# A causal depthwise convolution as three filters of half the taps, in a two-layer streaming encoder on one core

## The chip, the core and the metric

The kernel runs on one core of a Trainium2 chip. The metric is the device time of one execution in microseconds (us). The core has a matrix engine (TensorE, PE in the profile, with its weight loads as PEld), a vector engine (VectorE, DVE), an engine for functions of one input (ScalarE, ACT), a general engine (GpSimd, POOL) and a queue for transfers (SyncE, SP). Each executes its own list of instructions in order and waits at semaphores for the others.

## The reference, cut to what matters

One step of a two-layer encoder over 576 frames: 512 of a new stream and 64 of a running one. Each layer projects its input to queries, keys, values and the two inputs of a convolution, runs attention and the convolution, projects both back, normalizes, and runs a feed-forward part with a second norm. The part that the change touches is the causal depthwise convolution with 31 taps over 512 channels, and what follows it:

```
CONV_WIDTH = 31; CONV_HIST = CONV_WIDTH - 1

def causal_depthwise_conv(u, hist, w, b):
    full = jnp.concatenate([hist, u], axis=1)
    y = lax.conv_general_dilated(full, w[:, None, :], window_strides=(1,), padding='VALID', ...,
                                 feature_group_count=D_CONV)
    return y + b, full[:, -CONV_HIST:]
...
    u = ca * jax.nn.sigmoid(cg)
    c, conv_state = causal_depthwise_conv(u, hist, p['conv_w'][l], p['conv_b'][l])
    c = jax.nn.silu(layer_norm(c, p['conv_ln_g'][l], p['conv_ln_b'][l]))
    mix = jnp.concatenate([attn.reshape(B, T, D_ATTN), c], axis=-1)
    y = jnp.einsum('bte,ed->btd', mix, p['w_out'][l])
```

## The kernel before

Activations lie with the channels on the 128 partitions and the 576 frames along the free dimension, in two groups of 288. A weight of 128x1024 comes in float32 and is split into a high and a low part (`wh`, `wl`); a product is three matmuls (lines 734, 735, 736: high by high, high by low, low by high) on blocks of 128x128 by 128x288. `weights` makes the split: ACT copies the high part (line 891), and DVE or POOL subtracts it for the low part (line 894); or, where the running fraction `DM` says so, ACT writes the negative and the high part (lines 875 and 881), and a DMA from POOL's queue adds the weight to the negative (line 878). Layer 1's first 20 weights are split ahead, during layer 0's feed-forward part, and kept in memory (`split_ahead`).

Per layer the work is: 20 projection units (queries q, keys k, values v, and the gate g and input a of each of four channel tiles of the convolution); rotary products (lines 1367 to 1385); attention for four heads, five query blocks each (lines 1486 to 1574); the convolution of four channel tiles; its layer norm over channels (sum over tiles at line 1669, mean by a matmul at 1679, scale at 1725); the output projection with the residual (lines 1799, 1804, 1857, running sums at 1835); a layer norm (`layer_norm`: mean at 1029 and 1034, subtraction at 1052, squares on ACT at 1058 with sums on POOL at 1064, statistics at 1006); the feed-forward part by a scheme with fewer block products; and the second norm.

The convolution of a tile reads `ub`, 636 columns: 30 zeros, the 512 frames, 30 frames of history and the 64 frames. All 606 windows are computed for each tap. The first `NPT` taps go over ACT, which multiplies by the tap (lines 1319 and 1322), and POOL, which adds (line 1325) into a tile `r`. The other taps go over DVE: one instruction of 606 elements each multiplies and adds into an accumulator in PSUM (`sc`, line 1337, the first tap at 1335). Three additions join the two (line 1344).

The order of all instructions on PE, DVE, ACT, POOL and SP is made ahead, when the program is built, by a list scheduler (`Sched`). It gives each step a cost per engine (`cV`, `cA`, `cG`, `cP`, `cD`), a priority, and buffers to take and return, and it picks the engine where several can do a step. Its numbers per phase (`PHASES`, four phases in each layer) set priorities, penalties and choices, `NPT` among them.

Of the kernel before, what the change touches and what calls it, by code (L numbers as in the profile page):

```python
# [144 lines left out]
DL = 2.2  # L145
# [56 lines left out]
  'LD1': 0.76,
  'LD2': 0.58,
  'LD3': 1.12,
  'LDO': 113.7,
# [4 lines left out]
  'PA': 729.8,  # L210
  'PC': -623.4,
  'PCN': 616.8,
  'PE_': 162.9,
  'PK': -234.5,
# [2 lines left out]
  'PR': -253.2,
  'PS': 120.4,
  'PT': 791.6,
  'PV': 358.4,  # L220
# [101 lines left out]
 {'CH': 2,  # L322
  'CSTD': 2,
  'DM': 0,
# [4 lines left out]
  'LD1': 1.27,  # L329
  'LD2': 2.31,  # L330
  'LD3': 1.29,
  'LDO': -40.7,
# [1 line left out]
  'LP': -1.01,
  'LPE': 0.85,
  'LPT': -0.43,
  'NPT': '9,10,12,12',
# [1 line left out]
  'PC': -524.7,
  'PCN': 602.4,  # L340
  'PE_': 461.1,
  'PK': -255.4,
  'PN': -270.8,
# [2085 lines left out]
```

## Time and profile before

| | |
|---|---|
| median of 3 runs | 1374.9 us (1372.52 to 1377.28) |
| the profiled execution | 1375.67 us, span 1373.9 us |
| busy: PE, DVE, ACT, POOL | 1308.0, 1078.1, 705.1, 302.3 us |
| granted clock of TensorE, mean | 0.977 |

The span runs from the first to the last instruction; the execution's own time is 1.8 us longer. An engine's busy time is a sum over stages with different limits, so the stretches matter more than the shares: projection, attention and convolution take about 35 to 210 us in layer 0 and 700 to 875 us in layer 1, and the feed-forward parts about 300 to 665 and 960 to 1345 us. The granted clock is 1.00 or 0.50 at each moment, and its mean over a stretch says what part of it ran at half.

### The profile page before, as it was taken

The numbers are of one execution on the slowest core, as the hardware profiler recorded it, in microseconds if no ns is written. First come the engines' busy times: TensorE is split into PE (matmuls) and PEld (weight loads), VectorE is DVE, ScalarE is ACT, GpSimd is POOL, SyncE is SP. The second block draws the span as 40 slices with busy tenths as digits, with TensorE's granted clock in tenths as the row PEclk, the third lists the DMA queues.
The fourth block names the chain that finished last, engine by engine and source line by source line (L and its number), as shares of the span: only waits on it lengthen the run. The fifth ranks groups of instructions, "written<-read, shape, count | busy, mean of one in ns | idle before, by whom it ended". The sixth has DMA issues, their size and how long they took to land.

```text
span 1373.9 us, 24858 instructions
## 1 busy us (share of the span) xinstructions
PE 1308.0 (95%) x9518; PEld 1264.1 (92%) x9518; DVE 1078.1 (78%) x2206; ACT 705.1 (51%) x1413; POOL 302.3 (22%) x292
## 2 busy tenths in 40 slices
PE   8989989979999999999999999899989999999997
PEld 7878879979899999999998988798889999999996
DVE  5899998777888887878658999868677676767737
ACT  5766677265444444434156657754654443434424
POOL 0456620150000000000144885223400000000013
PEclk9999989989999999999999999899999999999998
DMA  6635533334465645554345444454234343435262
GB/s 220 162 94 140 122 117 106 93 130 156 144 211 165 208 168 192 185 167 139 102 158 204 160 152 121 129 135 118 64 79 117 112 108 108 124 80 144 70 152 69
DMA packets 70102, 186.38 MB, mean 136 GB/s; under 512 B 10848, under 2 KB 16608, under 8 KB 69984
## 3 DMA queue, kind: packets, MB, share of 16 engines
q1 hardware_dynamic: 63504, 161.20, 34.9%
q0 software_dynamic: 6480, 23.60, 10.4%
q8 instruction: 75, 1.23, 0.4%
q14 instruction: 43, 0.35, 0.1%
HBM read 154.11 MB, written 30.65 MB: 134 GB/s over the span
## 4 chain that ended last, share of the span: by engine, by line
PE 72%; DVE 18%; issue 3%; DMA 2%; ACT 2%; POOL 2%; SPq 0%; ACTq 0%; DVEq 0%; POOLq 0%
PE b L734 21%; PE b L735 21%; PE b L736 21%; DVE sc L1337 8%; DMA raw<-in_wu_dram 2%; PE sc L734 1%; PE b L1006 1%; POOL sq L1064 1%; PE sc L736 1%; PE b L1568 1%; PE sc L735 1%; DVE nm L1486 1%; DVE P L1530 1%; DMA wl<-in_wu_dram 1%; PE b L1611 1%
## 5 line engine op out<-in xcount | busy, mean ns | idle before, releaser
L734 PE MATMUL b<-x,wh 128*128 128x288 f32 x1356 | 416.2, 307 | 6.6 <-ACT wh L891 4.0
L736 PE MATMUL b<-x,wl 128*128 128x288 f32 x1356 | 406.1, 299 | 7.0 <-DVE wl L894 4.8
L735 PE MATMUL b<-x,wh 128*128 128x288 f32 x1356 | 406.5, 300 | 1.7 <-DVE x L1215 1.1
L734 PE MATMUL b<-a,wh 128*128 128x288 f32 x1088 | 325.0, 299 | 0.2 <-ACT x L731 0.2
L735 PE MATMUL b<-a,wh 128*128 128x288 f32 x1088 | 321.3, 295 | 0.0
L736 PE MATMUL b<-a,wl 128*128 128x288 f32 x1088 | 321.0, 295 | 0.0
L734 PEld LDWEIGHTS b<-x,wh 128*128 128x128 f32 x1356 | 260.5, 192 | 13.5 <-ACT wh L891 4.0
L736 PEld LDWEIGHTS b<-x,wl 128*128 128x128 f32 x1356 | 260.2, 192 | 8.2 <-DVE wl L894 5.3
L735 PEld LDWEIGHTS b<-x,wh 128*128 128x128 f32 x1356 | 260.6, 192 | 4.0 <-DVE x L1215 2.5
L734 PEld LDWEIGHTS b<-a,wh 128*128 128x128 f32 x1088 | 205.1, 188 | 2.0 <-issue 0.6
L735 PEld LDWEIGHTS b<-a,wh 128*128 128x128 f32 x1088 | 205.4, 189 | 0.5
L736 PEld LDWEIGHTS b<-a,wl 128*128 128x128 f32 x1088 | 205.1, 188 | 0.0
L2273 DVE TENSOR_TENSOR r<-r,b 128x288 f32<-128x288 f32 x192 | 85.7, 450 | 87.6 <-PE b L736 87.3
L1337 DVE SCALAR_TENSOR_TENSOR sc<-ub,par,sc 128x606 f32<-128x606 f32 x160 | 136.2, 851 | 4.2
L878 POOL DMA_DIRECT2D wl<-in_wu_dram x45 | 39.2, 871 | 446.8 <-ACT wl L875 387.6
L1064 POOL TENSOR_TENSOR sq<-sq,sq 128x288 f32<-128x288 f32 x40 | 35.7, 910 | 416.1 <-ACT sq L1058 415.5
L1325 POOL TENSOR_TENSOR r<-r,prod 128x606 f32<-128x606 f32 x72 | 113.7, 1580 | 54.8 <-ACT prod L1322 31.0
L891 ACT CAST wh<-raw 128x1024 fp32r<-128x1024 f32 (+1 forms) x73 | 71.4, 979 | 71.2 <-PE b L735 52.3
L2056 ACT CAST wh<-ckv 128x512 fp32r<-128x512 f32 x104 | 64.1, 620 | 76.7 <-PE b L735 61.2
L894 DVE TENSOR_TENSOR wl<-raw,wh 128x1024 fp32r<-128x1024 f32 (+1 forms) x73 | 84.5, 1161 | 22.3 <-ACT wh L891 21.7
L1884 DVE TENSOR_TENSOR wl<-ckv,wh 128x512 fp32r<-128x512 f32 x104 | 71.1, 685 | 6.0 <-ACT wh L2056 5.8
L875 ACT ACTIVATE wl<-raw 128x1024 fp32r<-128x1024 f32 x45 | 47.7, 1060 | 44.2 <-PE b L736 25.5
(320 smaller groups left out, 2409.9 us busy)
## 6 DMA issues: line engine op xcount, KB each, us to landing
raw<-in_wu_dram SPq DMA_DIRECT2D x110, 512.0 KB, 4.6
wl<-in_wu_dram POOLq DMA_DIRECT2D x45, 512.0 KB, 7.2
wscr<-cs SPq DMA_DIRECT2D x80, 256.0 KB, 2.0
ckv<-in_wu_dram SPq DMA_DIRECT2D x26, 512.0 KB, 3.6
ah<-in_wu_dram SPq DMA_DIRECT2D x26, 512.0 KB, 4.4
cs<-in_wu_dram SPq DMA_DIRECT2D x40, 256.0 KB, 2.8
wh<-wscr SPq DMA_DIRECT2D x20, 512.0 KB, 3.3
wl<-wscr SPq DMA_DIRECT2D x20, 512.0 KB, 4.4
```

Of the source, the lines that this page charges most:

```text
L734: TE.matmul(o, wh, xh, start=start, stop=False)
L735: TE.matmul(o, wh, xl, start=False, stop=False)
L736: TE.matmul(o, wl, xh, start=False, stop=stop)
L875: S.activation(wt["lo"], wt["raw"], AF.Copy, scale=-1.0)
L891: S.copy(wt["hi"][:, c], wt["raw"][:, c])
L894: e.tensor_tensor(wt["lo"][:, c], wt["raw"][:, c], wt["hi"][:, c].bitcast(F32), op=ALU.subtract)
L1064: e.tensor_tensor(q[a]["t"], q[a]["t"], q[b]["t"], op=ALU.add)
L1325: GP.tensor_tensor(cc[t], cc[t], st[j], op=ALU.add)
L1337: V.scalar_tensor_tensor(st["a0"], win(j), w, st["a0"], op0=ALU.mult, op1=ALU.add)
L1884: e.tensor_tensor(o, a, b, op=ALU.subtract)
L2056: S.copy(tl["wh"][box["i"]][:, off:off + n], src())
L2273: V.tensor_tensor(rr, rr, bk(), op=ALU.add)
```

## The change

The convolution is computed with even and odd frames apart. With U0 and U1 the even and odd columns of `ub` (318 each), H0 the 16 even taps and H1 the 15 odd taps, it makes A = H0 on U0, B = H1 on U1 (with the bias), and C = (H0 + H1) on U0 + U1; the even outputs are A + B, and the odd ones C - A - B, with B taken one column later. That is 16 + 15 + 16 = 47 filters' taps over 303 or 304 columns, in place of 31 taps over 606, which is 62 in the same unit. B is made by ACT (products) and POOL (sums); `NPT` is at least 15 in the phases that use it, so all of B goes there. A and C are made on DVE, in the two banks of the same PSUM tile `sc`. C starts from the negative of A, which lies there. The sum U0 + U1 is a step for DVE or POOL. The results lie with the even outputs first, and the copies behind the convolution's norm put them back in order. `ub` is returned when A, B and U0 + U1 are made.

The scheduler's numbers are changed in all eight phases, with three of its constants (`PD`, `DL`, the cost of the first loads of x). The core of the diff:

```
-  'DM': 0.67,
+  'DM': 1,
...
-  'NPT': '9,9,9,10',
+  'NPT': '15,15,15,15',
...
+            taps = pr[:, P_CW:P_CB].rearrange("p (t w) -> p t w", w=W)
+            V.tensor_tensor(cv[:, :, 1:], taps[:, :, 2::2], taps[:, :, 1::2], op=ALU.add)
+            V.tensor_scalar(cv[:, :, 0], pr[:, P_CB:P_CG], 2.0, None, op0=ALU.mult)
...
+            def frames(odd, i, n):
+                return ub[t].rearrange("p (n two) -> p two n", two=2)[:, odd, i:i + n]
+            def b_(n=YH + 1, o=0):
+                return cc[t][:, UH + o:UH + o + n]
...
-                        S.activation(st[j], ub[t][:, j:j + UC], AF.Copy, scale=w)
+                        S.activation(st[j], frames(1, j, YH + 1), AF.Copy, scale=w)
...
-                    GP.tensor_tensor(cc[t], cc[t], st[j], op=ALU.add)
+                    GP.tensor_tensor(b_(), b_(), st[j], op=ALU.add)
...
+                e.tensor_tensor(cc[t][:, :UH], frames(0, 0, UH), frames(1, 0, UH), op=ALU.add)
+            sm = op({"V": cV(UH), "G": cG(UH)}, both, (*start, cc["n", t]), pri=PT)
...
-            for j in range(npt, W):
+            for j in range(W // 2 + 1):
...
-                        V.scalar_tensor_tensor(st["a0"], win(j), w, st["a0"], op0=ALU.mult, op1=ALU.add)
-                vt = op({"V": cV(UC, True) + 0.06}, va, (*start, pd, vt), acq=("cv", "sc") if j == npt else (), pri=PT)
+                        V.scalar_tensor_tensor(st["a"], frames(0, j, YH), w, st["a"], op0=ALU.mult, op1=ALU.add)
+                vt = op({"V": cV(YH, True)}, va, (*start, pd, vt), acq=("cv", "sc") if j == 0 else (), pri=PT)
...
+            for j in range(W // 2 + 1):
+                def vc(e, j=j):
+                    w = cv[:, t, j:j + 1] if j else pr[:, cw:cw + 1]
+                    V.scalar_tensor_tensor(st["c"], cc[t][:, j:j + YH], w, st["c"] if j else st["a"], op0=ALU.mult,
+                                           op1=ALU.add if j else ALU.subtract)
+                vt = op({"V": cV(YH, True)}, vc, (sm, vt, ld_n), pri=PT)
...
+                for o, i, n in ((0, 0, SEQ // 2), (SEQ // 2, S0 // 2, DEC // 2)):
+                    V.tensor_tensor(cc[t][:, o:o + n], st["a"][:, i:i + n], b_(n, i), op=ALU.add)
+                for o, i, n in ((0, 0, SEQ // 2), (SEQ // 2, S0 // 2, DEC // 2)):
+                    V.scalar_tensor_tensor(cc[t][:, T // 2 + o:T // 2 + o + n], st["c"][:, i:i + n], cv[:, t, 0:1],
+                                           b_(n, i + 1), op0=ALU.add, op1=ALU.subtract)
...
-                copy(e, cmix[t][0], cc[t][:, :T])
+                copy(e, halves(cmix[t][0]), cc[t][:, :T].rearrange("p (two n) -> p two n", two=2))
```

What the new numbers do to the order is seen in the instruction lists. VectorE in layer 0, the middle of the first tile's convolution, before (`ub` the tile's input, `par` the taps, `nm`, `rc` and `P` of attention):

```order
L1337 SCALAR_TENSOR_TENSOR sc_119<-ub_544,par_161,sc_119 128x2x303 x3
L1485 MEMSET sc_118 64x2x64
L1486 TENSOR_REDUCE nm_594<-sc_118 128x2
L1337 SCALAR_TENSOR_TENSOR sc_119<-ub_544,par_161,sc_119 128x2x303 x7
L1485 MEMSET sc_118 64x2x64
L1486 TENSOR_REDUCE nm_595<-sc_118 128x2
L1337 SCALAR_TENSOR_TENSOR sc_119<-ub_544,par_161,sc_119 128x2x303 x2
```

and now, from the end of the even filter into the summed one (`r` holds U0 + U1, `cv` the summed taps):

```order
L1524 TENSOR_REDUCE nm_588<-sc_118 128x2
L1367 SCALAR_TENSOR_TENSOR sc_119<-ub_538,par_161,sc_119 128x303 x2
L736 COPY ah_99<-b_117 128x128
L1374 SCALAR_TENSOR_TENSOR sc_119<-r_91,par_161,sc_119 128x303
L1374 SCALAR_TENSOR_TENSOR sc_119<-r_91,cv_165,sc_119 128x303
L1555 RECIPROCAL rc_593<-sums_587 128x2
L1556 TENSOR_TENSOR rc_593<-rc_593,nlam_162 128x1
L1374 SCALAR_TENSOR_TENSOR sc_119<-r_91,cv_165,sc_119 128x303 x2
L1568 SCALAR_TENSOR_TENSOR P_659<-P_659,rc_593 128x256
```

The taps are more instructions and half as wide, and attention's steps stand between them as before.

PE in layer 0 at the mean of the convolution's norm (`sgm` by `ones_h`), before; `x` by `wh` or `wl` are matmuls of the projection:

```order
L734 MATMUL b_115<-x_185,wh_85 128x288
L735 MATMUL b_115<-x_186,wh_85 128x288
L736 MATMUL b_115<-x_185,wl_89 128x288
L1539 MATMUL b_114<-ident,P_1783 128x128 x3
L1679 MATMUL sc_118<-sgm_101,ones_h 128x288 x2
L734 MATMUL b_115<-x_171,wh_85 128x288
L735 MATMUL b_115<-x_172,wh_85 128x288
L736 MATMUL b_115<-x_171,wl_89 128x288
```

and now:

```order
L740 MATMUL b_115<-a_1542,a_1299 128x64
L741 MATMUL b_115<-a_1541,a_1300 128x64
L1606 MATMUL b_116<-ah_99,a_1480 128x256 x3
L1606 MATMUL b_116<-ah_99,a_1480 128x128
L1717 MATMUL sc_118<-sgm_101,ones_h 128x288 x2
L739 MATMUL b_117<-x_181,wh_83 128x288
L740 MATMUL b_117<-x_182,wh_83 128x288
L741 MATMUL b_117<-x_181,wl_87 128x288
```

The mean stands after 806 matmuls of 288 columns instead of 890. In layer 1 it is 5102 instead of 5150, counted from the start of the program.

VectorE around the first layer norm of layer 0, before, from the last subtractions of the second group (`b_115` is its mean) to its statistics (`lrv`):

```order
L1052 TENSOR_TENSOR r_93<-r_93,b_115 128x288
L1052 TENSOR_TENSOR r_96<-r_96,b_115 128x288
L1052 TENSOR_TENSOR r_91<-r_91,b_115 128x288
L894 TENSOR_TENSOR wl_87<-raw_81,wh_83 128x1024
L894 TENSOR_TENSOR wl_88<-raw_82,wh_84 128x1024
L819 TENSOR_TENSOR cs_3077<-cs_3077 128x512
L959 TENSOR_SCALAR lrv_2936<-b_115 96x3
```

and now, from the last subtractions of the first group (`b_117`) to its statistics:

```order
L1066 TENSOR_TENSOR r_96<-r_96,b_117 128x288
L1066 TENSOR_TENSOR r_97<-r_97,b_117 128x288
L1838 SCALAR_TENSOR_TENSOR r_92<-r_92,b_114 128x288
L1838 SCALAR_TENSOR_TENSOR r_96<-r_96,b_116 128x288
L908 TENSOR_TENSOR wl_87<-raw_81,wh_83 128x1024
L1838 SCALAR_TENSOR_TENSOR r_97<-r_97,b_115 128x288
L1843 TENSOR_TENSOR r_96<-r_96,x_2494 128x288
L973 TENSOR_SCALAR lrv_3058<-b_117 96x3
```

The low part of the first feed-forward weight (`wl_87`) stood behind the second group's subtractions and now stands ahead of the first group's statistics. The second unit's low part (`wl_88`), which stood beside it, is now made by the accumulating DMA.

Counted over the whole program, DVE has 44 weight splits of 128x1024 instead of 65, POOL issues 66 accumulating DMAs instead of 45, and ACT has 66 negatives instead of 45 and as many high parts as before. In layer 0, ahead of its first norm: ten of those splits on DVE become five; seven more of the rotary steps at lines 1370, 1371 and 1385 stand on DVE and as many fewer on POOL; the 13 residual additions at line 1804 and the six sums at line 1835 that stood on DVE stand on POOL. In layer 1's same part, nine more additions, products and subtractions of 512 or 576 columns stand on DVE that stood on POOL, with two products of 64 columns.

More of the change, by code (lines that the diff above doesn't have):

```diff
@@ L197 @@
   'DM': 0.67,
-  'KA': 7,
-  'KB': 1,
-  'KR': 7,
+  'KA': 5,
+  'KB': 7,
+  'KR': 8,
   'LA': 0.18,
[L202 to L205, printed above, removed]
+  'LD1': 2.02,
+  'LD2': 1.02,
+  'LD3': 0.81,
+  'LDO': 257.5,
   'LDS': 800,
   'LP': 1.63,
-  'LPE': 1.21,
+  'LPE': 0.42,
   'LPT': 0.33,
[L210 to L214, printed above, removed]
+  'PA': 621.7,
+  'PC': -693.7,
+  'PCN': 610.1,
+  'PE_': -449.0,
+  'PK': -168.4,
   'PN': 345.0,
   'PQ': 26.4,
[L217 to L220, printed above, removed]
+  'PR': -558.7,
+  'PS': 158.5,
+  'PT': 686.6,
+  'PV': 381.1,
   'PW': -111.3,
   'PX': 313.8,
-  'QL0': '0 6 7',
+  'QL0': '0 2 4 6 7',
   'QL1': '0 6',
-  'QLF': '0 6 7',
+  'QLF': '0 6',
   'RG': 1,
-  'RP': [3],
+  'RP': [0, 3, 4],
   'RS': 1,
-  'S2F': [3, 5],
-  'S2H': [4, 5],
+  'S2F': [0, 3, 5, 7],
+  'S2H': [3, 4, 5],
   'SH': ['d1'],
   'SHP': 0,
-  'VP': 0.2,
+  'VP': 0.97,
   'VS': 3.23,
   'WP': 3.13,
-  'WP2': -0.39,
+  'WP2': -0.69,
   'WP3': 0.44},
@@ L328 @@
   'LA': 0.36,
[L329 to L332, printed above, removed]
+  'LD1': 2.0,
+  'LD2': 2.73,
+  'LD3': 2.2,
+  'LDO': -237.9,
   'LDS': 800,
[L334 to L337, printed above, removed]
+  'LP': -1.98,
+  'LPE': 0.79,
+  'LPT': 0.68,
+  'NPT': '16,15,15,15',
   'PA': 632.1,
[L339 to L343, printed above, removed]
+  'PC': -254.4,
+  'PCN': 613.0,
+  'PE_': 426.9,
+  'PK': -383.0,
+  'PN': -324.2,
   'PR': 0.0,
-  'PS': -6.5,
+  'PS': 80.6,
   'PT': 755.3,
-  'PV': 636.9,
-  'PW': 87.5,
+  'PV': 770.3,
+  'PW': -709.0,
   'PX': -121.8,
@@ L369 @@
   'KB': 7,
-  'KR': 1,
-  'LA': 1,
+  'KR': 6,
+  'LA': 0.85,
   'LD1': 2.07,
   'LD2': 0.86,
-  'LD3': 1.49,
-  'LDO': -165.8,
-  'LP': 0.9,
-  'LPE': 1.52,
+  'LD3': 1.74,
+  'LDO': -165.5,
+  'LP': 0.96,
+  'LPE': 1.96,
   'LPT': 0.22,
@@ L421 @@
   'PCN': 826.0,
-  'PE_': 317.9,
-  'PK': -148.1,
-  'PN': 12.5,
-  'PQ': -26.3,
+  'PE_': 437.1,
+  'PK': -299.6,
+  'PN': -180.3,
+  'PQ': -37.8,
   'PR': -255.5,
-  'PS': -541.0,
-  'PT': 1328.5,
-  'PV': -307.5,
-  'PW': 222.2,
-  'PX': -295.5,
+  'PS': -386.2,
+  'PT': 1272.9,
+  'PV': -557.0,
+  'PW': 373.7,
+  'PX': 424.9,
   'QL0': '0 4 6 7',
   'QL1': '0 6',
-  'QLF': '0 2 4 6 7',
+  'QLF': '0 6 7',
   'RG': 0,
-  'RP': [1, 3, 4, 5],
+  'RP': [3, 4, 5, 6],
   'RS': 1,
-  'S2F': [1, 3, 7],
+  'S2F': [3, 7],
   'S2H': [4, 7],
-  'VP': -0.0,
-  'VS': 1.91,
-  'WP': -1.53,
-  'WP2': -1.19,
+  'SHP': 0,
+  'VP': -0.95,
+  'VS': 2.61,
+  'WP': -2.2,
+  'WP2': -1.85,
   'WP3': 0.12},
- {'CS': 1,
+ {'CH': 3,
+  'CS': 1,
   'CSTD': 2,
-  'DM': 1,
+  'DM': 0.34,
   'KA': 1,
@@ L476 @@
   'RG': 0,
-  'RP': [],
-  'RS': 1,
+  'RP': [5],
+  'RS': 0,
   'S2F': [0, 3, 4, 5],
@@ L746, in xt, with halves @@
         return take("x")
+    def halves(z):
+        return z.rearrange("p (n two) -> p two n", two=2)
     def at(dt=F32R):
@@ L763, in params @@
         ch = cp.tile([128, 2 * CT], F32, name=f"ch{l}")
+        cv = cp.tile([128, CT, W // 2 + 1], F32, name=f"cv{l}")
         prs.append(pr)
@@ new lines, in conv, with vb, both @@
+            for j in range(npt, W // 2):
+                def vb(e, j=j):
+                    V.scalar_tensor_tensor(b_(), frames(1, j, YH + 1), pr[:, cw + 2 * j + 1:cw + 2 * j + 2], b_(),
+                                           op0=ALU.mult, op1=ALU.add)
+                pg = op({"V": cV(YH, True)}, vb, (*start, pd, pg), pri=PT, two=True)
+            def both(e):
+                e.tensor_tensor(cc[t][:, :UH], frames(0, 0, UH), frames(1, 0, UH), op=ALU.add)
+            sm = op({"V": cV(UH), "G": cG(UH)}, both, (*start, cc["n", t]), pri=PT)
```

236 lines of the change are left out of this document (118 added, 118 removed).

## The prediction

> **What bounds the kernel now.** The page comes first: span, busy shares, the chain that ended last.
>
> ```profile
> span 1373.9 us, 24858 instructions
> PE 1308.0 (95%) x9518; PEld 1264.1 (92%) x9518; DVE 1078.1 (78%) x2206; ACT 705.1 (51%) x1413; POOL 302.3 (22%) x292
> ...
> PE 72%; DVE 18%; issue 3%; DMA 2%; ACT 2%; POOL 2%; SPq 0%; ACTq 0%; DVEq 0%; POOLq 0%
> PE b L734 21%; PE b L735 21%; PE b L736 21%; DVE sc L1337 8%; DMA raw<-in_wu_dram 2%; PE sc L734 1%; PE b L1006 1%; POOL sq L1064 1%; PE sc L736 1%; PE b L1568 1%; PE sc L735 1%; DVE nm L1486 1%; DVE P L1530 1%; DMA wl<-in_wu_dram 1%; PE b L1611 1%
> ```
>
> TensorE is the bound on average, and the convolution's VectorE instruction (L1337) holds 8% of the chain. Where each counts, the table by stretches says (columns: stretch, its length, busy time and count of PE, PEld, DVE, ACT, POOL, granted clock, DMA share, GB/s).
>
> ```profile
> 105.00:140.00 35.00, 31.84 (x231) 31.37 (x230) 33.79 (x48) 24.01 (x39) 26.58 (x21) 0.95 0.59 142
> 140.00:175.00 35.00, 33.06 (x232) 30.71 (x231) 33.82 (x62) 22.79 (x53) 21.13 (x17) 0.95 0.49 120
> 175.00:210.00 35.00, 31.08 (x205) 25.86 (x203) 31.25 (x75) 26.25 (x66) 8.43 (x7) 0.85 0.40 119
> 210.00:245.00 35.00, 35.00 (x254) 32.80 (x253) 28.86 (x68) 24.86 (x60) 1.74 (x2) 1.00 0.40 110
> 280.00:315.00 35.00, 28.89 (x182) 28.02 (x181) 24.74 (x50) 21.20 (x48) 17.97 (x20) 0.80 0.42 143
> 455.00:490.00 35.00, 35.00 (x267) 35.00 (x266) 31.77 (x65) 15.97 (x29) 0.00 (x0) 1.00 0.55 189
> 770.00:805.00 35.00, 34.16 (x263) 33.78 (x263) 33.85 (x52) 19.12 (x35) 30.14 (x24) 1.00 0.50 173
> 840.00:875.00 35.00, 30.81 (x200) 26.75 (x198) 31.13 (x70) 24.42 (x63) 14.66 (x12) 0.88 0.50 129
> ```
>
> At 455 us (feed-forward) PE issues 267 matmuls in 35 us, 0.131 us each, without a gap: there only fewer matmuls would help, and the change removes none. At 105 to 175 us (projection, attention and convolution of layer 0) and at 770 us (layer 1) DVE is busy 33.8 of 35 us: VectorE is the bound. Behind it lie tails (175 and 840 us) where PE has too little ready, and the first layer norm of layer 0 (280 us) with a clock of 0.80. So the change can only gain in these stages.
>
> **The convolution on VectorE.** The rows that price it (in the first four: count, busy us, mean ns):
>
> ```profile
> L1337 DVE SCALAR_TENSOR_TENSOR sc<-ub,par,sc 128x606 f32<-128x606 f32 x160 | 136.2, 851 | 4.2
> L894 DVE TENSOR_TENSOR wl<-raw,wh 128x1024 fp32r<-128x1024 f32 x65 | 81.2, 1251 | 21.3 <-ACT wh L891 20.9
> L1804 DVE TENSOR_TENSOR r<-r,x 128x288 f32<-128x288 f32 x32 | 15.6, 491 | 0.9
> L1835 DVE TENSOR_TENSOR sg<-sg,r 128x288 f32<-128x288 f32 x34 | 16.1, 473 | 1.0
> 769.48 10.64 DVE L1337 SCALAR_TENSOR_TENSOR sc<-ub,par,sc 128x606 f32<-128x606 f32 x12
> 781.09 0.87 DVE L1344 TENSOR_TENSOR r<-r,sc 128x303 f32<-128x303 f32 x3
> 190.87 0.47 DVE L1530 SCALAR_TENSOR_TENSOR P<-P,rc 128x256 f32<-128x256 f32 x1
> 221.09 0.75 DVE L1530 SCALAR_TENSOR_TENSOR P<-P,rc 128x512 f32<-128x512 f32 x1
> ```
>
> Twelve taps in a row take 10.64 us, 0.887 each: 0.851 and a gap of 0.036, since each tap reads what the one before wrote. L1530 is the same operation, also with its factor in a column of SBUF: 0.75 at 512 elements and 0.47 at 256, so 1.09 ns per element. A tap of 303 elements is then 0.887 - 303 x 0.00109 = 0.557 us, not half. Removed on DVE: 31 taps less those that ACT and POOL take, 22+22+22+21 = 87 in layer 0 and 22+21+19+19 = 81 in layer 1: 77.2 and 71.8 us. Added: 16 taps of the even filter and 16 of the summed one per tile, 128 per layer: 71.3 us. The closing additions are four in place of three (0.87): about 1.1 us, 4 x 0.23 = 0.9 us more per layer. So DVE's convolution changes by -5.0 us in layer 0 and +0.4 us in layer 1. "47 for 62" counts elements; the fixed part per instruction eats the rest. The least that a tap can take is half, 0.44 us (-19 and -15 us).
>
> The frames are now read two elements apart. No row of this trace has such a read on DVE; it is free, or at worst doubles the 303 x 1.09 ns = 0.33 us of the 64 even taps of a layer, +21 us per layer, 42 in all. I take zero: L1337 and L1530 both go at about one element per ns, which needs no neighbour fetched along with it, and the gain below zero is excluded since a strided read fetches no less. The Trainium skill, SBUF — State Buffer, section on the DMA port swizzle, says that two accesses to one 16-byte line keep the full rate, and a step of 8 bytes makes two; no run here shows it.
>
> A rule speaks against the change: the Trainium skill, Perfetto Trace Analysis, section Optimizing Scalar/DVE Operations, says that larger operations pay where an engine is saturated, with a fixed 125 ns for DVE on PSUM. The trace agrees in direction and its fixed part is larger (0.887 - 606 x 0.00109 = 0.23 us). By the page's figure, an estimate, 88 more instructions would cost 11 us instead of 20 in both layers together.
>
> **ACT and POOL in the convolution.**
>
> ```profile
> L1325 POOL TENSOR_TENSOR r<-r,prod 128x606 f32<-128x606 f32 x72 | 113.7, 1580 | 54.8 <-ACT prod L1322 31.0 <-issue 20.8
> L1154 POOL TENSOR_TENSOR x<-r,x 128x288 fp32r<-128x288 f32 x48 | 39.9, 852 | 43.1 <-ACT x L731 41.4 <-DVE r L1052 1.2
> L1322 ACT ACTIVATE prod<-ub,par 128x606 f32<-128x606 f32 x72 | 56.7, 801 | 11.9 <-POOL r L1325 11.5
> L1058 ACT ACTIVATE sq<-r 128x288 f32<-128x288 f32 x64 | 25.4, 440 | 60.9 <-DVE r L1052 59.6 <-POOL sq L1064 0.9 <-PE b L736 0.4
> L1370 DVE TENSOR_TENSOR swp<-swp,cs 128x576 f32<-128x576 f32 x6 | 4.5, 755 | 0.1
> ```
>
> POOL: 72 sums of 1.58 (114 us) become 112 of about 0.90 (L1154 scaled to 304), 101 us, and six even-plus-odd sums. Per tile that is a row of 14 x 0.90 = 12.6 us beside 32 x 0.557 = 17.8 us on DVE; the closing addition still waits for DVE, so POOL costs nothing. ACT: 112 products between 0.44 (L1058) and 0.80; I take 0.55, 62 us for 57, under a 51% engine.
>
> **What the new order moves on VectorE.** Counted in the two orders. Layer 0, ahead of the last closing addition and just behind: five weight splits go to ACT and the accumulating DMA (5 x 1.25 = -6.3 us), seven rotary products and subtractions come from POOL (7 x 0.755 = +5.3), and small pieces (+2). Later, 13 residual adds and 6 sums go to POOL (13 x 0.491 + 6 x 0.473 = -9.2). Layer 1: products and splits come from POOL, about +6 us, and nothing leaves. Demand on DVE, with the convolution: layer 0 -13 us, layer 1 +6 to +7.
>
> How that becomes time is seen at the channel mean of the convolution (L1679), which starts its layer norm, and at the sum that it needs (L1669):
>
> ```profile
> 162.75 0.75 DVE L1669 TENSOR_TENSOR sgm<-sgm,r 128x576 f32<-128x576 f32 x1
> 170.97 1.14 PE L1679 MATMUL sc<-sgm,ones_h 128*128 128x288 f32 x4
> 836.80 0.75 DVE L1669 TENSOR_TENSOR sgm<-sgm,r 128x576 f32<-128x576 f32 x1
> 837.93 1.24 PE L1679 MATMUL sc<-sgm,ones_h 128*128 128x288 f32 x4
> ```
>
> Layer 0: the sum is there at 163.5, the mean runs at 170.97. It stood 7.5 us in PE's queue behind projection matmuls. Now 806 matmuls of 288 columns are ahead of it instead of 890: 84 x 0.131 = 11 us earlier. The layer norm starts up to 7.5 us sooner, the tail has 84 more matmuls to run beside attention, and in that tail (175 to 210) PE did 205 of 267 with the clock at 0.85. I take -8 us; ends: 0 (the 84 matmuls are only missing earlier) and -13 (all of DVE's relief).
>
> Layer 1: the sum is ready at 837.55 and the mean runs 0.4 us later; DVE is the late one. DVE has 6 us more to do, and the mean stands 48 matmuls (6.3 us) earlier in PE's queue, so PE stands at it up to 12 us; the 48 matmuls behind it give 6.3 back in the tail. I take +5; ends 0 and +12.
>
> **The first layer norm of layer 0.**
>
> ```profile
> 283.44 3.21 DVE L894 TENSOR_TENSOR wl<-raw,wh 128x1024 fp32r<-128x1024 f32 x2
> 284.97 0.61 PE L736 MATMUL b<-x,wl 128*128 128x288 f32 x1 [4.83 <-DVE wl L894]
> 289.31 2.08 PE L1006 MATMUL b<-ones_c,sq 128*96 128x1 f32 x12 [1.28 <-POOL sq L1064]
> L1835 POOL TENSOR_TENSOR sg<-sg,r 128x288 f32<-128x288 f32 x3 | 2.4, 800 | 4.9 <-DVE r L1857 4.4 <-DVE sg L1835 0.4
> ```
>
> PE stands 4.83 us because the splits of the first feed-forward weights come behind the eight subtractions of the second group; after that it runs at half clock (0.80 over 35 us is 7 us lost). Now the first split stands ahead of the first group's statistics, the second unit is split by DMA, and three units instead of two run beside the norm. The 4.83 go, and some of the clock. Next late is POOL: the running sums for the means now stand wholly on it, 0.80 each for DVE's 0.473, six in a row, so the mean can come 6 x 0.33 = 2 us later, and low parts of x and the DMA split queue there too. I take -5; ends +2 and -11.
>
> Elsewhere (start, feed-forward, second layer norms, end) PE's order hardly changes. More splits by DMA in layer 0's feed-forward take DVE work from a stretch where PE has no gap: 0, with +-3 for the joints.
>
> Sum: -8 + 5 - 5 = -8 on the profiled execution of 1375.7 us (1.8 around its span), which is 0.8 above the median of 1374.9. A saving this small counts alike on both: 1367 against the median.
>
> **Rivals.** *Slower:* PE, in order, stands at the layer 0 mean too. It needs the last closing addition, and ahead of that DVE loses only 5.0 + 6.3 - 7.3 = 4 us. If those 4 are lost in waits, the sum comes at 163.5 again, PE arrives 11 us earlier than its 171, and waits 3.5 us; if DVE rather than PE sets the tail, the 84 matmuls return nothing. Layer 0 is then +4, layer 1 +10, the layer norm -5: 1384. It decides from a sum later than 160 us on. For it: DVE at 33.8 of 35 us. Against it: PE at 31.1 of 35 in the tail behind. Strided reads at half rate end here too (42 us of DVE, some 25 in time, 1400).
>
> *No change:* layer 0 gains 4, layer 1 loses 6, the layer norm gains 2: 1375.
>
> *Much faster:* a tap of half the length takes half (0.44). DVE then has 128 x 0.117 = 15 us less per layer than in my sum: layer 1 turns from +6 to -9 of demand, of which I count 4, and layer 0 gains its 13 us in full: -13 - 4 - 5 = -22, 1353. Against it: L1530.
>
> **How the numbers follow.** About 0.3% (4.1 us) is what a measurement here tells from no change. Forecast (-4 to -16 us, 1359 to 1371): 0.39. Much faster (1345 to 1359): 0.14. No change (1371 to 1379): 0.24. Slower (1379 to 1400): 0.23, of it 0.04 for the strided reads. Faster 0.53, same 0.24, slower 0.23. The range leaves out about 1 in 10 on each side: 1350 to 1384; the forecast's own is 1359 to 1371.
>
> **What would show it.** Right: taps of 0.52 us with gaps of 0.04; the layer 0 mean before 168 us and the stretch at 175 with more than 205 matmuls; no 4.8 us wait at the first feed-forward weight; a wait of PE at layer 1's mean. Wrong: taps under 0.46 or over 0.7 us; a wait of PE over 4 us at layer 0's mean; waits for splits by DMA in layer 0's projection, where all units now take that way.

## The result, and the profile after

The changed kernel takes 1396.4 us (median of 4 runs, 1394.44 to 1401.5) against 1374.5 of the kernel before (1372.52 to 1377.28): ratio 1.0163, 95% interval 1.0131 to 1.0196. It is 22 us slower; 8 us faster was forecast. The profiled execution is the slowest of its four (1401.5 us), so its stages add up to about 4 us more than the medians differ by.

The page of the changed kernel, its span and busy times:

```profile
span 1399.7 us, 25237 instructions
...
PE 1319.7 (94%) x9530; PEld 1275.7 (91%) x9530; DVE 1063.3 (76%) x2326; ACT 706.8 (50%) x1413; POOL 295.0 (21%) x370
```

VectorE has 15 us less to do (1078.1 before), and the kernel is longer. The table by stretches, changed kernel, columns as before:

```profile
105.00:140.00 35.00, 31.58 (x219) 30.58 (x218) 27.46 (x59) 23.59 (x51) 16.03 (x22) 0.90 0.62 149
140.00:175.00 35.00, 29.18 (x190) 26.82 (x189) 31.90 (x63) 23.27 (x53) 16.16 (x19) 0.90 0.35 86
175.00:210.00 35.00, 31.48 (x222) 27.81 (x220) 33.35 (x68) 22.32 (x50) 9.85 (x9) 0.95 0.42 107
280.00:315.00 35.00, 29.76 (x210) 27.93 (x210) 26.16 (x66) 23.74 (x51) 23.58 (x30) 0.95 0.49 136
770.00:805.00 35.00, 31.37 (x235) 30.26 (x234) 33.43 (x76) 21.75 (x51) 17.23 (x24) 1.00 0.37 126
```

(The columns after the length are busy time and count of PE, PEld, DVE, ACT and POOL, then the granted clock, the DMA share and GB/s.) At 105 us VectorE is busy 27.5 of 35 us (33.8 before): it has idle time now. PE does 219 and 190 matmuls in the first two stretches, 231 and 232 before. VectorE got time free in this stage, and the stage got slower. The instructions of the convolution by shape (count, busy us, mean ns):

```profile
L1345 POOL TENSOR_TENSOR r<-r,prod 128x304 f32<-128x304 f32 x112 | 84.8, 757 | 49.6 <-ACT prod L1342 44.5 <-POOL r L1345 0.3
L1367 DVE SCALAR_TENSOR_TENSOR sc<-ub,par,sc 128x303 f32<-128x303 f32 x120 | 64.4, 537 | 3.4
L1374 DVE SCALAR_TENSOR_TENSOR sc<-r,cv,sc 128x303 f32<-128x303 f32 x120 | 64.4, 537 | 3.4
L1342 ACT ACTIVATE prod<-ub,par 128x304 f32<-128x304 f32 x112 | 61.2, 568 | 7.7 <-POOL r L1345 7.3
```

The even taps (L1367) read every second column, the summed taps (L1374) read columns side by side: they take 537 ns both.

To see where the time goes, the span is cut at rows that both kernels have. The first cut is the mean of layer 0's first layer norm (line 1029 before, 1043 now), before and after (start us, us, what):

```profile
262.83 0.65 PE L1029 MATMUL b<-sg,ones_d 128*128 128x288 f32 x2
```

```profile
274.72 0.65 PE L1043 MATMUL b<-sg,ones_d 128*128 128x288 f32 x2
```

Projection, attention and convolution of layer 0 end 11.9 us later. The next cuts are that norm's second broadcast, the end of layer 0, layer 1's mean, and its second broadcast. Three of the six stretches, before and then after, as windows (start:end, length, busy times, clock, DMA share, GB/s): layer 0 up to the mean, layer 1 likewise, layer 1's first norm.

```profile
0.00:262.80 262.80, 239.27 (x1656) 222.68 (x1657) 222.72 (x429) 168.85 (x356) 95.21 (x88) 0.95 0.51 138
704.10:936.80 232.70, 221.36 (x1579) 205.78 (x1577) 197.49 (x379) 141.73 (x318) 113.89 (x95) 0.97 0.50 152
936.80:968.90 32.10, 27.97 (x199) 25.50 (x199) 25.22 (x67) 18.79 (x38) 16.98 (x20) 1.00 0.41 100
```

```profile
0.00:274.70 274.70, 244.07 (x1656) 226.55 (x1657) 214.64 (x467) 173.59 (x381) 97.20 (x129) 0.94 0.54 141
715.80:954.10 238.30, 223.25 (x1580) 209.29 (x1578) 196.65 (x442) 144.70 (x337) 81.94 (x101) 0.96 0.48 148
954.10:991.90 37.80, 32.81 (x199) 30.94 (x200) 25.09 (x67) 18.88 (x38) 16.45 (x20) 0.82 0.33 84
```

PE does the same 1656 matmuls in layer 0's stretch, VectorE works 8 us less, and it takes 11.9 us longer: PE's own busy time grows by 4.8 us (239.27 to 244.07, at a lower mean clock) and its idle time by 7.1. Layer 1 takes 5.6 more, its norm 5.7 more. Where PE stands, between 30 and 275 us (engine and line, waited for: us in all, times, longest), before and after:

```profile
PE b L1541 <- DVE P L1530: 4.4, 1, 4.4
PE b L1539 <- DVE P L1530: 4.3, 3, 1.9
PE sc L734 <- DVE r L1344: 3.2, 1, 3.2
PE sc L734 <- ACT P L1502: 2.4, 1, 2.4
```

```profile
PE sc L739 <- ACT P L1540: 6.8, 4, 2.8
PE b L1577 <- ACT r L1398: 5.5, 1, 5.5
PE b L1577 <- DVE P L1568: 4.4, 4, 1.8
PE sc L739 <- ACT a L736: 3.1, 1, 3.1
PE b L1579 <- DVE P L1568: 3.0, 1, 3.0
```

PE now waits for ACT, a 50% engine, at the scores (L739 into `sc`) and at attention's transposes (L1577). The longest wait, with what stood ahead of it:

```profile
155.24 2.82 DVE L1374 SCALAR_TENSOR_TENSOR sc<-r,cv,sc 128x303 f32<-128x303 f32 x5
157.97 0.16 DVE L1555 RECIPROCAL rc<-sums 128x2 f32<-128x2 f32 x1
158.16 0.72 ACT L1562 ACTIVATE P<-P,rc 128x512 f32<-128x512 f32 x1 [4.27 <-DVE rc L1555]
158.16 0.16 DVE L1556 TENSOR_TENSOR rc<-rc,nlam 128x1 f32<-128x1 f32 x1
158.24 3.40 DVE L1374 SCALAR_TENSOR_TENSOR sc<-r,cv,sc 128x303 f32<-128x303 f32 x6
158.79 1.03 ACT L895 CAST wh<-raw 128x1024 fp32r<-128x1024 f32 x1
159.73 0.39 ACT L1398 COPY r<-b 128x288 f32<-128x288 f32 x1
160.17 0.90 PE L1577 MATMUL b<-ident,P 128*128 128x128 f32 x3 [5.54 <-ACT r L1398]
```

VectorE runs five taps, then a reciprocal of two columns that attention needs; ACT stands 4.27 us for that reciprocal, and behind it in ACT's order, after a weight's copy (L895), is the copy (L1398) that empties the PSUM bank PE wants; PE stands 5.54 us. Here the theory starts. The planner puts small attention steps between taps by its own price of a tap, `cV(303)` = 0.07 + 303 x 0.00104 = 0.385 us. The trace has 2.82 / 5 = 0.564. For the kernel before, the price was 0.07 + 606 x 0.00104 + 0.06 = 0.760 us, and the trace has 0.887. Over the price VectorE took 87 x 0.127 = 11 us in layer 0 before, and takes 128 x 0.18 = 23 us now.

### The profile page after: what moved, and what is told of

It is laid out like the page before. It is cut to its first block, busy times and chain, and to the rows that moved or that the text cites. A ratio compares the mean times of both kernels' runs of the same rounds, so it can differ in the third digit from the quotient of the medians.

```text
span 1399.7 us, 25237 instructions
## 1 busy us (share of the span) xinstructions
PE 1319.7 (94%) x9530; PEld 1275.7 (91%) x9530; DVE 1063.3 (76%) x2326; ACT 706.8 (50%) x1413; POOL 295.0 (21%) x370
## 5 line engine op out<-in xcount | busy, mean ns | idle before, releaser
L739 PE MATMUL b<-x,wh 128*128 128x288 f32 x1356 | 420.8, 310 | 8.8 <-ACT wh L905 5.2
L739 PE MATMUL b<-a,wh 128*128 128x288 f32 x1084 | 325.3, 300 | 2.6 <-ACT ah L736 1.1
L739 PEld LDWEIGHTS b<-x,wh 128*128 128x128 f32 x1356 | 263.3, 194 | 16.4 <-ACT wh L905 4.2
L741 PEld LDWEIGHTS b<-x,wl 128*128 128x128 f32 x1356 | 263.4, 194 | 5.5 <-DMA wl<-in_wu_dram 4.2
L740 PEld LDWEIGHTS b<-x,wh 128*128 128x128 f32 x1356 | 263.5, 194 | 3.2 <-POOL x L1168 1.5
L892 POOL DMA_DIRECT2D wl<-in_wu_dram x66 | 57.6, 872 | 830.8 <-ACT wl L889 527.4
L739 PEld LDWEIGHTS b<-a,wh 128*128 128x128 f32 x1084 | 205.0, 189 | 6.0 <-ACT ah L736 1.3
L889 ACT ACTIVATE wl<-raw 128x1024 fp32r<-128x1024 f32 x66 | 69.8, 1058 | 53.4 <-PE b L741 32.8
L1345 POOL TENSOR_TENSOR r<-r,prod 128x304 f32<-128x304 f32 x112 | 84.8, 757 | 49.6 <-ACT prod L1342 44.5
L905 ACT CAST wh<-raw 128x1024 fp32r<-128x1024 f32 (+1 forms) x52 | 49.3, 951 | 72.2 <-PE b L740 47.1
L908 DVE TENSOR_TENSOR wl<-raw,wh 128x1024 fp32r<-128x1024 f32 (+1 forms) x52 | 58.1, 1122 | 23.4 <-ACT wh L905 22.8
L895 ACT CAST wh<-raw 128x1024 fp32r<-128x1024 f32 x66 | 68.6, 1039 | 0.0
L1367 DVE SCALAR_TENSOR_TENSOR sc<-ub,par,sc 128x303 f32<-128x303 f32 x120 | 64.4, 537 | 3.4
```

What stands on the lines that cost most here:

```text
L739: TE.matmul(o, wh, xh, start=start, stop=False)
L740: TE.matmul(o, wh, xl, start=False, stop=False)
L741: TE.matmul(o, wl, xh, start=False, stop=stop)
L889: S.activation(wt["lo"], wt["raw"], AF.Copy, scale=-1.0)
L892: GP.dma_start(wt["lo"], wu[l, i], accum_op=ALU.add)
L895: S.copy(wt["hi"], wt["raw"])
```

## The experiments

Theory 1: the taps' time over the planner's price makes every step behind them late, in engines that work in order. Theory 2: the new form of the convolution costs by itself. Theory 3: the 66 weight splits by DMA (45 before) come late. Theory 4: the new numbers give a worse order for any convolution. Each kernel's median, its ratio to the kernel before with the interval, and stage lengths from its profile (L0: start to layer 0's mean; N0: to that norm's second broadcast; F0: to the end of layer 0; L1: from there to layer 1's mean; N1: to that norm's second broadcast; then the rest). Each stage length is of one profiled run, which can lie up to 6 us off the median:

| kernel | median us | ratio (95%) | L0 | N0 | F0 | L1 | N1 | rest |
|---|---|---|---|---|---|---|---|---|
| before | 1374.5 | | 262.8 | 34.3 | 407.0 | 232.7 | 32.1 | 405.0 |
| changed | 1396.4 | 1.0163 (1.0131 to 1.0196) | 274.7 | 31.5 | 409.6 | 238.3 | 37.8 | 407.8 |
| new numbers, old convolution | 1414.0 | 1.0281 (1.022 to 1.0341) | 266.5 | 33.3 | 420.7 | 241.4 | 37.4 | 409.6 |
| new convolution, old numbers | 1388.5 | 1.0099 (1.0074 to 1.0124) | 272.8 | 32.9 | 408.6 | 236.3 | 31.8 | 404.7 |
| changed, taps at 215 columns | 1370.5 | 0.9992 (0.9971 to 1.0013) | 256.8 | 31.6 | 407.8 | 226.7 | 38.1 | 407.5 |
| changed, taps at 128 columns | 1360.2 | 0.9881 (0.983 to 0.9932) | 248.5 | 32.3 | 408.1 | 220.5 | 38.2 | 407.7 |
| changed, taps at 64 columns | 1357.4 | 0.9889 (0.9869 to 0.991) | 251.5 | 32.0 | 408.8 | 221.4 | 34.9 | 406.3 |
| before, taps at 480 columns | 1376.6 | 0.9999 (0.997 to 1.0029) | 264.3 | 34.2 | 406.4 | 234.7 | 33.4 | 403.7 |
| changed, true price | 1402.4 | 1.022 (1.0191 to 1.0249) | 265.7 | 33.0 | 427.2 | 235.1 | 34.6 | 410.7 |
| new convolution, old numbers, true price | 1373.9 | 1.0000 (0.9981 to 1.0018) | 262.4 | 32.2 | 410.3 | 228.8 | 31.9 | 408.5 |
| the same, taps at 128 columns | 1373.0 | 1.0002 (0.9985 to 1.002) | 259.0 | 32.1 | 410.0 | 232.0 | 33.3 | 409.6 |
| new convolution, old numbers, taps at 128 columns | 1348.4 | 0.9815 (0.9789 to 0.9841) | 251.7 | 34.2 | 406.5 | 220.1 | 31.9 | 403.7 |
| changed, old numbers in N1 | 1400.4 | 1.0201 (1.0169 to 1.0234) | 273.5 | 31.3 | 407.7 | 236.7 | 32.9 | 410.2 |
| true prices, table fitted anew | 1412.6 | 1.0312 (1.0272 to 1.0352) | 263.8 | 37.6 | 436.0 | 229.6 | 31.1 | 411.0 |

Where kernels share an order, stretches without an edit repeat within 1 to 3 us between profiles.

**The halves of the change.** First the new numbers on the old convolution (its `NPT` stays):

```
  PHASES, PD, DL, PRP, PRS, first loads of x: as in the changed kernel
-  'NPT': '15,15,15,15',
+  'NPT': '9,9,9,10',
   conv(): as before
```

> The new table of numbers, and the planner's new constants, with the old convolution (62 taps); only the taps' split between ACT/POOL and DVE keeps the old counts. Theory 1 (the planner prices a half-width tap at 0.385 us where the trace has 0.56, so every step queued behind taps on DVE comes late): the old tap was priced at 0.76 us for 0.887, so this kernel's unpriced time on DVE is the old 168 x 0.127 = 21 us and not 256 x 0.175 = 45 us; it lands near the kernel before, 1370 to 1385 us. Theory 2 (the new form of the convolution costs by itself, in any order): the same 1370 to 1385. Theory 3 (the additional weight splits that come by DMA, 66 for 45, with their later landings): those come with the numbers, so 1388 or more. Theory 4 (the new numbers give a worse order whatever the convolution is): 1390 or more.

Measured: 1414.0 us, 39 more than before, where the whole change costs 22. Then the new convolution with the old numbers (`NPT` at 15 or 16):

> The new convolution (47 half-width taps) under the old table of numbers and the old constants; the count of odd taps on ACT/POOL is 15 as in the changed kernel. Theory 1: 45 us of unpriced DVE time in a planned order as in the changed kernel, 1385 to 1405 us. Theory 2: likewise 1385 to 1405. Theories 3 and 4 (the numbers are at fault): 1380 or less, since the old numbers are back.

Measured: 1388.5 us. Against theories 3 and 4, the loss is mostly there without the new numbers, +10.0 us in L0 and +3.6 in L1. Where PE stands most in it, between 30 and 275 us:

```profile
PE b L1573 <- DVE P L1564: 10.4, 7, 4.1
```

That is attention again: seven times PE waits for an attention step of VectorE (L1564). But theory 1's figure for the first half was wrong by 29 us, where theories 3 and 4 had 1388 and 1390 or more: the numbers are fitted to one plan, and under another convolution they cost 14 us in F0 alone, where no convolution is. So of the 22 us the new convolution makes 14 under the old numbers, and the new numbers add some 8, of which 5.7 are N1's (N1 takes 37.4 us with them on the old convolution, 31.8 without them).

**Taps that take what the planner thought.** Every instruction keeps its place on every engine; 240 of the taps get shorter and leave the columns behind the 128th out of their sums.

```
-   V.scalar_tensor_tensor(st["a"], frames(0, j, YH), w, st["a"], ...)
+   V.scalar_tensor_tensor(st["a"][:, :128], frames(0, j, 128), w, st["a"][:, :128], ...)
...
-   V.scalar_tensor_tensor(st["c"], cc[t][:, j:j + YH], w, ...)
+   V.scalar_tensor_tensor(st["c"][:, :n], cc[t][:, j:j + n], w, ...)      # n = 128 if j else YH
```

> The changed kernel with every instruction at its place, but 240 of its DVE taps cover 128 columns and not 303 (the other columns are left out of the sums), which by the slope between the two widths of the traces (851 ns for 606, 537 ns for 303: 1.04 ns a column) makes each 0.18 us shorter, so about 0.38 us from one to the next, the planner's own price. Theory 1: PE's lost time in layer 0's projection, attention and convolution stage falls from 62.7 us by 10 to 16, layer 1's by 5 to 10, and the whole goes from 1396 to 1366 to 1380 us. Theory 2 would also have some of that if the DVE time is what costs, but not if it is the number of instructions and semaphores: then 1388 to 1396. Theories 3 and 4: 1388 to 1396, since order, transfers and numbers are those of the changed kernel.

Measured: 1360.2 us, 36 less than the changed kernel and 6 more than the most that was forecast: L0 -26.2, L1 -17.8, the rest as it was (the profiled runs differ by 44 us, the medians by 36). The same place in its trace:

```profile
133.89 1.91 DVE L1374 SCALAR_TENSOR_TENSOR sc<-r,cv,sc 128x128 f32<-128x128 f32 x5
135.71 0.16 DVE L1555 RECIPROCAL rc<-sums 128x2 f32<-128x2 f32 x1
136.01 2.30 DVE L1374 SCALAR_TENSOR_TENSOR sc<-r,cv,sc 128x128 f32<-128x128 f32 x6
136.63 0.71 ACT L1562 ACTIVATE P<-P,rc 128x512 f32<-128x512 f32 x1
138.18 0.39 ACT L1398 COPY r<-b 128x288 f32<-128x288 f32 x1
138.62 0.55 PE L1577 MATMUL b<-ident,P 128*128 128x128 f32 x3 [1.07 <-ACT r L1398]
```

Five taps in 1.91 us (0.382 each, the price), ACT is no longer waiting when the reciprocal comes, and PE stands 1.07 us where it stood 5.54. Theory 3 falls here for the bulk of the loss: the same 66 splits come by DMA. The dose, half of the time over the price (215 in place of 128 in the edit) and then less than the price (64):

> As before with 215 columns in 240 taps: half of the time over the price is taken away, 240 x 0.092 = 22 us of DVE. Both theories: about half of the gain that the taps at the price gave (36 us by the medians), 1373 to 1383 us. If the gain has a threshold (the clock's dips go only when nearly all stalls are gone), it is much less than half, 1385 or more, or much more, 1368 or less.

> As the kernel with the taps at 128 columns, every instruction at its place, but 64 columns in 240 taps (the rest left out of the sums): by the slope of the two widths run before, (537 - 354) / 175 = 1.05 ns a column, 0.287 us a tap, 0.067 less than at 128, so 16 us less again, and shorter than the planner's price. Theory 1 (the time over the price is what delays): the gain stops at the price, 1355 to 1361 us against 1360 at 128 columns. Rival A (DVE's work bounds these stages whatever the plan says): the gain goes on at nearly one for one, 1344 to 1351.

Measured: 1370.5 and 1357.4 us. From 303 to 215 columns 22 us of VectorE bring 26 us, from 215 to 128 the same 22 us bring 10, and from 128 to 64, below the price, 16 us bring 3. The first lies between the two forecasts (1373 to 1383, and 1368 or less), the second where theory 1 had it; in L0 and L1 together the step to 64 columns brings nothing (469.0 us at 128, 472.9 at 64). So the gain stops about where the price lies, as theory 1 says, and it is not a straight line above it: the first half of the lateness costs less than half of its own time, the second half more than all of it. Part of this is the clock (last section). The control on the kernel before:

```
-   V.scalar_tensor_tensor(st["a0"], win(j), w, st["a0"], ...)
+   V.scalar_tensor_tensor(st["a0"][:, :, :240], win(j)[:, :, :240], w, st["a0"][:, :, :240], ...)
```

> The control: the kernel before with its 160 DVE taps cut from 606 to 480 columns (the rest left out of the sums), so that each takes about 0.72 busy and 0.76 us from one to the next, its planner's price, where it was 0.851 and 0.887. 160 x 0.13 = 21 us of DVE time go. Theory 1 in its narrow form (the unpriced time is what delays): half the changed kernel's excess was there before too, so 3 to 10 us are gained, 1364 to 1372. If less DVE time in general is what helps, without regard to the planner, the gain is as large as that of the shortened changed kernel for each us removed, 1360 to 1366. If DVE's time is not what PE waits for in the kernel before: 1372 to 1376.

Measured: 1376.6 us, no gain. The taps fell from 851 to 720 ns; the 21 us over the price that they took before cost nothing. So theory 1 in its narrow form falls (not every us over the price costs), and the time of VectorE's taps was not what PE waited for in the kernel before: L0 takes 264.3 us with VectorE busy 213.2 us there, and took 262.8 with 222.7. Part of the reason is in the waits of the closing addition, here of this control:

```profile
its engine sat idle before it (us, times) until:
  POOL r L1325: 3.3, 2
```

VectorE reaches the addition earlier and then stands 3.3 us for POOL's sums (0.5 us with the full taps).

**The price told to the planner.**

```
-   vt = op({"V": cV(YH, True)}, va, ...)
+   vt = op({"V": cV(YH, True) + 0.175}, va, ...)       # and the same for vc
```

> The new convolution under the old table of numbers (1388 us with the tap at 0.385) with the tap priced at 0.56 us. Theory 1: 1370 to 1383 us. Rival A (DVE full): 1385 to 1398. Rival B (a table fits the price that it was made for; the old one was made for an old tap priced within 0.13 of the truth): as theory 1, and better than the same price under the new table.

> The changed kernel, its whole work, with one thing told to the planner: a half-width tap is priced at 0.56 us, as the trace has it from one tap to the next, and not at 0.385. The planner writes another order; the table of numbers stays. Theory 1 (the wrong price is the cause): the order leaves DVE the time that the taps take, attention's small steps are no longer behind unforeseen taps, 1370 to 1388 us. Rival A (DVE is simply full in these two stages in the new form, and no order hides its 256 taps): 1392 to 1405. Rival B (the table fits the wrong price only): slower than 1405.

Measured: 1373.9 us under the old numbers, 14.6 less than with the short price, and 1402.4 under the new ones, no better. The first is as theory 1 had it, with the whole work done: L0 262.4 us with VectorE busy 213.6 us there, where the changed kernel took 274.7 us with 214.6 busy. The same work is hidden once the plan knows of it. The wait for VectorE's step at L1564 that was 10.4 us with the short price (at L1573) is 0.8 us here; the largest waits between 30 and 262 us are

```profile
PE sc L735 <- ACT P L1536: 2.8, 3, 1.3
PE b L1575 <- DVE P L1564: 2.0, 1, 2.0
```

The second, as a whole, landed where rival A had it (1392 to 1405). The stages speak against rival A: L0 and L1, the only ones with taps, gain 9.0 and 3.2 us as theory 1 says, and F0 loses 17.6 in the feed-forward part, without any tap. That is near to rival B, but it is not the price alone that the table fits: under the old convolution the new numbers have the same wait of 4.0 us at the line shown below and an F0 of 420.7. The table fits the one plan that it was made for. One place of it, a wait and the windows around it:

```profile
347.61 0.58 PE L739 MATMUL sc<-a,wh 128*128 128x288 f32 x1 [3.95 <-DVE r L2310]
```

```profile
340.00:345.00 5.00, 3.66 (x28) 3.42 (x26) 1.79 (x5) 0.62 (x1) 0.00 (x0) 1.00 0.46 157
350.00:355.00 5.00, 4.08 (x16) 3.38 (x15) 1.76 (x4) 0.06 (x1) 0.00 (x0) 0.50 0.00 0
365.00:370.00 5.00, 4.28 (x17) 3.61 (x15) 2.17 (x5) 0.04 (x1) 0.00 (x0) 0.50 0.53 152
375.00:380.00 5.00, 5.00 (x39) 5.00 (x39) 5.00 (x11) 5.00 (x10) 0.86 (x1) 1.00 0.57 143
```

PE stands 3.95 us for VectorE, and then its clock is at half for over 20 us: 16 or 17 matmuls in 5 us instead of 39. In the changed kernel the wait for the same line is 0.64 us there at most.

Whether the 14.6 us are the price's or the mere reordering's is answered by shortening the taps in both plans in place (the edit is that of the 128 columns):

> The mirror of the taps at the planned price: the kernel with the old numbers and the tap priced at 0.56 us (1374 us), every instruction at its place, and 240 DVE taps cut to 128 columns (the rest left out of the sums). The same 44 us of DVE time go as in the changed kernel, where that gave 36 us; but this plan had left room for them. Theory 1 (what delays is time over the price): 0 to 12 us gained, 1362 to 1374. Rival A (DVE's work as such bounds the two stages in the new form): 25 to 40 us gained, 1334 to 1349.

> The new convolution under the old numbers with the tap priced at 0.385 us (1388 us), every instruction at its place, and 240 DVE taps cut to 128 columns (the rest left out of the sums), so that each takes what the planner thought. It tells whether the 14.5 us by which the same kernel with the true price is faster come from the price or from the other order that any change of a price brings. Theory 1: the taps' time over the price costs in this plan too, 14 us or more are gained, 1360 to 1375 us. If the other order alone made the difference: 1380 to 1389.

Measured: 1373.0 us, 1 us gained, in the plan made with the true price, and 1348.4 us, 40 us gained, in the plan made with the short price. The second gains more than was forecast (1360 to 1375). Same convolution, same numbers, the same 44 us taken off the taps: they are worth nothing where the plan had left room and 40 us where it had not. That is theory 1, shown in a plan other than the one it was formed on; rival A (VectorE's work as such bounds the stage) is ruled out for the plan with the true price. The 14.6 us are what is left of the 40: the plan that leaves room for the taps is itself 25 us longer (1373.0) than the other would be if the taps were short (1348.4).

**The rest.** Layer 1's first norm with its block of the table put back:

```
  PHASES[5] (layer 1, first norm): the numbers of before
  the seven other blocks and conv(): as in the changed kernel
```

> The changed kernel with one block of the table put back: the numbers of layer 1's first layer norm (its junction took 37.8 us from the mean to the second broadcast, 32.1 before, and 31.8 with the whole old table). If the 5.7 us come from that block: the junction takes 31 to 34 us and the whole 1389 to 1394. If they come from what the stage before hands over (late landings, the order that the convolution leaves behind): 36 to 39 us and 1394 to 1399.

Measured: N1 32.9 us in the profile, 1400.4 us in all (1394.1 to 1403.2; the profiled run is the fastest). The block is the cause of N1's length, as the 32.9 us beside 37.8 say; that the kernel gains by it is not shown, its median is 4 us above the changed kernel's. Last, a kernel meant to be faster than both:

```
   conv() and its prices: new convolution, taps + 0.175
-   a = op({"A": cA(YH, 1 if j else 2)}, pa, ...)
+   a = op({"A": cA(YH, 1 if j else 2) + 0.12}, pa, ...)
   PHASES: fitted anew, from the old numbers
```

> The new convolution, its whole work, with the tap priced at 0.56 us, ACT's product at 0.56 (0.12 more than the planner had), and the table of numbers fitted anew to these prices: about 7000 small random changes to the old table, kept when the planner's own makespan, meaned over these prices and over DVE and ACT prices 5% higher, went down. By the planner's makespan the plan is 21 us shorter than the one that it starts from, whose twin (without the price of ACT's product) took 1374 us. Theory 1 (with true prices the plan is what the chip does): some half to all of the 21 us come, 1352 to 1365 us, faster than both kernels. Rival (a table fitted to the planner's makespan fits its remaining errors, as the changed kernel's did): 1370 to 1385.

Measured: 1412.6 us, the opposite, and slower than even the rival had it (1370 to 1385). L0 and L1 are as good as with the old numbers at the true price (263.8 and 229.6 us), but F0 takes 436.0 and N0 37.6. With tap and product priced right, the fit seems to have gone after the planner's other errors; which ones no run shows. The two largest waits of PE in that F0 (its lines stand 23 further down than the changed kernel's):

```profile
PE b L762 <- DVE sq L2224: 8.7, 6, 2.8
PE b L762 <- DVE r L2335: 4.5, 5, 1.5
```

No version here beats the kernel before with the whole work done; the new convolution under the old numbers and the true price equals it.

## Why the prediction was wrong

**The failed step is "how that becomes time" in layer 0's projection, attention and convolution stage: -8 us forecast (ends 0 and -13), +11.9 measured.** I read "busy 33.8 of 35 us" as "VectorE is the bound", counted what VectorE has to do, found less of it, and turned the relief into time. The demand did fall, by 8.1 us (222.7 to 214.6 busy; 13 forecast). Two things were wrong. The relief was not worth time: 9 us less of VectorE in this stage moved it by +1.5 us in the kernel before with shorter taps and by -0.4 us in the new convolution under the old numbers and the true price (262.4 us). And a cost was left out, at nothing: the planner had priced these taps at 0.385 us. The diff shows it: `cV(UC, True) + 0.06` became `cV(YH, True)`, and the row L1530 that gave me 0.557 also said that this was 0.17 short. I priced the taps for the chip and never asked what the plan believed. The runs put it in numbers, under the old numbers: 272.8 us with the short price, 262.4 with the true one. In the changed kernel's own plan the stage takes 248.5 us with taps at the price and 274.7 over it.

**The rival for slower had the sign and the wrong place.** It had PE standing at the convolution's mean. The sum and the mean in both layers, changed kernel:

```profile
164.60 0.96 DVE L1707 TENSOR_TENSOR sgm<-sgm,r 128x576 f32<-128x576 f32 x1
168.70 1.14 PE L1717 MATMUL sc<-sgm,ones_h 128*128 128x288 f32 x4
857.14 0.76 DVE L1707 TENSOR_TENSOR sgm<-sgm,r 128x576 f32<-128x576 f32 x1
858.30 1.24 PE L1717 MATMUL sc<-sgm,ones_h 128*128 128x288 f32 x4
```

In layer 0 the sum is there 3.1 us ahead of the mean: PE does not stand there. The mean runs 2.3 us earlier than before where 84 fewer matmuls ahead of it were to bring 11, so PE had lost some 9 us by then: it stands in attention, at steps between the taps.

**Layer 1's +5 came out at +5.6, for another reason.** VectorE's demand there did not rise by 6 us (197.5 before, 196.7 after), and PE does not stand longer at the mean, which runs 0.4 us behind the sum as before; the stage became 17.8 us shorter when the taps were cut to the price. The agreement is luck.

**Layer 0's first norm, -5 forecast, gave -2.8.** The 4.83 us at the first split went, as said, and PE then stands 3.5 us at the statistics for POOL's squares: POOL is next late, as said, at another of its steps.

**"Elsewhere 0 +-3" missed N1**, +5.7 us, from its block of numbers, and 5 us more in F0 and the rest of the profiled run.

**The prices were right, but for POOL's.** A tap takes 0.564 us with its gap (0.557 forecast), the reads two elements apart cost nothing (537 ns either way), ACT's products take 568 ns (550) and POOL's sums 757 (900). The Trainium skill, SBUF — State Buffer, section on the DMA port swizzle, was cited for two accesses to a 16-byte line; the trace agrees, 537 and 537 ns. "47 for 62 counts elements" holds too: with the true price in the plan the new form is worth nothing (ratio 1.0000).

## What to carry to other kernels

Where a planner fixes the order, compare its price of each changed instruction with the trace before asking which engine is relieved: an instruction that takes longer than planned can delay what stands behind it, on engines that are half idle as well; it need not, as the 21 us in the kernel before show. Shortening the instructions in place, at an unchanged order, tells work that bounds from work that the plan did not expect: 44 us of taps were worth 40 us in one plan and 1 us in the other. A table fitted to a planner's makespan, the length that the planner computes for its own plan, can fit the planner's errors, so its gains count only when measured (21 us planned, 39 us lost).

## What the runs showed of the hardware

The fixed part of a dependent tap on VectorE with its accumulator in PSUM: 288, 354, 445 and 537 ns at 64, 128, 215 and 303 columns lie on 0.22 us + 1.04 ns a column, and about 0.03 us pass between two. The same operation with all its tiles in SBUF (L1530: 0.47 us at 256, 0.75 at 512 columns) has 0.20 to 0.22 us by that slope, so the accumulator's place does not explain it. The Trainium skill, Perfetto Trace Analysis, section Optimizing Scalar/DVE Operations, gives 125 ns of engine-busy time on PSUM and says that the latency seen in a profile is about twice that. Twice is 0.25 us, an estimate from that figure, and the trace's 0.22 to 0.25 us agrees; the prediction took the 125 ns alone and found the trace larger.

A wait can cost more than its length, through the clock. After 3.95 us without work (changed kernel, true price) PE ran at half speed for over 20 us, though it was busy 4.1 to 4.3 of 5 us in the two windows shown; the window without a gap has 1.00 again. After the 5.54 us of the changed kernel it ran at half speed for about 6 us, from 160 to 166, though it then worked without a wait. The Trainium skill, TensorE: Matmul & The Clock Gate, Part 1: The HAM clock gate, says that the clock halves after an idle window of about 3.4 us and returns after a busy one of the same length; the first half agrees with the row; for the second, windows that are 82 to 86% busy (4.08 and 4.28 of 5 us) did not bring it back here. These rows do not contradict the Trainium skill's rule: PE waited 0.55 us about every 3.8 us there (rows of the same trace), so it was never busy for much more than 3.2 us at a time. In layer 0's stage of the changed kernel's plan the mean clock was 0.94 with full taps, 0.98 at 215 columns, 0.99 at 128 and 0.97 at 64. The stage at 128 columns, to be read beside the changed kernel's row above:

```profile
0.00:248.50 248.50, 233.43 (x1656) 217.33 (x1657) 191.38 (x467) 172.64 (x381) 96.90 (x129) 0.99 0.59 156
```

For the same 1656 matmuls PE is busy 233.43 us here and 244.07 with full taps, and idle 15.1 and 30.6 us. By that, an estimate since the ends of matmuls are modelled, some 11 of the 26.2 us gained are slower matmuls and some 16 are standing; by the mean clock the first part is about (0.99 - 0.94) x 275 = 14 us. No run could hold the clock, so the two parts are not separated by an experiment.
